# A two-layer decoder trunk on one core: element-wise work on another engine, and a plain down product in the last part of a feed-forward block

## The chip, the cores and the metric

One core of one Trainium2 chip runs the whole program. The metric is the device time of one execution in microseconds; less is better. Five engines work side by side, each in the order of its own queue, and wait for each other by semaphores: TensorE (PE in the profile; PEld is its loading of weights), VectorE (DVE), ScalarE (ACT), GpSimd (POOL) and SyncE (SP), which here only issues transfers. GpSimd can issue transfers too.

## The reference

A trunk of two layers on 512 positions of width 1024, in float32. Each layer is a feed-forward block, a group of token mixers, cross-attention into 256 memory positions, and a second feed-forward block.

```python
for l in range(DEPTH):                                    # DEPTH = 2
    x = x + 0.5 * swiglu(rms_norm(x, ffn1_norm[l]), w_gate, w_up, w_down)      # D_FF = 2816
    h = rms_norm(x, mix_norm[l])
    a_val, a_gate, b_gate, c_gate, b_h, q, k, v, q_idx, k_idx, w_idx = split(h @ w_in[l])
    y_a = conformer_conv(a_val, a_gate, ...)              # causal convolution over 31, layer norm
    y_b = short_gated_conv(b_gate, c_gate, b_h, ...)
    q, k, q_idx, k_idx = rope(q), rope(k), rope(q_idx), rope(k_idx)
    y_c = dsa_attention(q, k, v, q_idx, k_idx, w_idx)     # each position attends to its top 128 keys
    x = x + concat(y_a, y_b, y_c) @ w_out[l]
    x = x + memory_cross_attention(rms_norm(x, xa_norm[l]), rms_norm(mem, mem_norm[l]), ...)
    x = x + 0.5 * swiglu(rms_norm(x, ffn2_norm[l]), w_gate, w_up, w_down)
return rms_norm(x, final_norm)

def rms_norm(x, g): return x * rsqrt(mean(x * x) + 1e-6) * g
def swiglu(h, w_gate, w_up, w_down): return (silu(h @ w_gate) * (h @ w_up)) @ w_down
def rope(t): t1, t2 = halves(t); return concat(t1 * c - t2 * s, t2 * c + t1 * s)
```

## The kernel before

**Layout and precision.** Channels lie on the 128 partitions and the 512 positions on the free axis, so x is eight tiles X[0] to X[7] of 128 x 512 (line 483). A product in float32 is made of three fast passes: `split` (397) writes a rounded copy of a tile ("hi", by ScalarE) and the remainder ("lo", by VectorE), and `mm3` (410) adds hi·hi, hi·lo and lo·hi. Weights go the same way: a transfer into `stg`, then ScalarE writes `whi` and VectorE writes `wlo`. There are four buffers each of `stg`, `whi` and `wlo`, and two of `sum`.

**Feed-forward block (`ffn`, 624).** The 22 chunks of the hidden width are worked off in three parts of 8, 8 and 6 (`PARTS`, 48): a part makes its chunks (gate, up, silu, product) and then multiplies them down into X. Except for the first four chunks, these products use the scheme of Strassen and Winograd: two by two blocks of operands are combined so that seven products of 256 columns replace eight. `load_sevens` (541) brings the weights: three transfers on SyncE's queue, two on GpSimd's that add to what lies in the buffer, two additions on VectorE, and four splits. `Sevens.add` (588) combines the other operand with four operations on VectorE and four splits. `seven` (629) runs the products A to G, and the function `three` (746) and `fourth` (753) bring the results from PSUM into X with seven operations of 256 columns on VectorE and three copies on ScalarE for a pair of output chunks. The plain way is there too: with `by_sevens` false (665) the hidden chunks go into `Whole` (605), which only splits them, `load_quarters` (565) brings a chunk's weights with one transfer and one split, and each output chunk is 6 x 3 products of 512 columns and one operation that adds it to X (729 to 737). Before the change this path is taken in the last part of the last block of the kernel alone.

**Norms (`Norm`, 485).** As soon as a chunk of X is final, `chunk` (493) lets ScalarE square it, splits it with the gain for the next stage's product, and adds the square to a running sum (line 511, GpSimd). The next stage starts to multiply at once; `finish` and `rstd` (454) make 1/rms from the sum by products with ones, a power on GpSimd and a broadcast, and the result is multiplied in behind the product. The memory's norm (`mem_norm`, 817) does the same with four tiles inside the first block.

**Token mixers (`mix`, 886).** Projections run on TensorE one behind the other. Each of the eleven tiles per layer that take rope goes through `rope` (944) and `rotate` (911): ScalarE copies it out of PSUM, SyncE issues four transfers that swap its halves into a second tile, GpSimd multiplies that tile by the sines (912), VectorE multiplies the first by the cosines and adds the two (913, 914). Then `doubled` (917) copies heads between partitions by three transfers, and splits follow. Meanwhile VectorE works off the top-k search and the 31 taps of the convolution in the background (`some`). The attention of four pairs of heads, the memory's keys and values (`mem_kv`) and the output projection (`out_proj`, 865) follow; the latter multiplies plainly, and each chunk goes through `Norm.chunk`.

**Order.** Nothing is issued as it is written. `Plan` records every operation with a price (`price`, 238: GpSimd 0.1 us + 2.2 ns for each column, VectorE 0.068 us + 1/960 us for each) and the delay until other engines see it (`SEEN`, 178), gives each a due time counted back from TensorE's work, and issues all engines in the order of a simulated run (`order`, 270). Each engine keeps this order on the chip. So a changed price or engine can change the order of neighbours as well.

Of the kernel before, what the change touches and what calls it, by code (L numbers as in the profile page):

```python
# [361 lines left out]
def trunk_kernel(ctx: ExitStack, tc: tile.TileContext, a: dict, out: bass.AP):  # L362
# [6 lines left out]
    nc = Plan(tc)  # L369
# [15 lines left out]
    def slot(dt=F32, w=T):  # L385
        return planned(slots, "s", T, dt)[:, :w]
# [10 lines left out]
    def split(src, hi=None, lo=None, scale=None):  # L397

        w = src.shape[-1]
        if hi is None:  # L400
            hi, lo = slot(F32R, w), slot(F32R, w)
        if scale is None:
            nc.scalar.activation(hi, src, AF.Copy)
            nc.vector.tensor_sub(lo, src, f(hi))
        else:
            nc.scalar.activation(hi, src, AF.Copy, scale=scale)
            nc.vector.scalar_tensor_tensor(lo, src, scale, f(hi), op0=ALU.mult, op1=ALU.subtract)
        return hi, lo
# [41 lines left out]
    def pcol(name, i):  # L450
        return cols[:, COLS[name] + i:COLS[name] + i + 1]


    def rstd(sq, n, eps, rb=None, broadcast=True):


        nb = sq[0].shape[-1] // P
        ps = bank()
        for j in range(nb):
            for i, s in enumerate(sq):  # L460
                nc.tensor.matmul(ps[:, j:j + 1], s[:, j * P:(j + 1) * P], ones[:, 0:1],
                                 start=i == 0, stop=i == len(sq) - 1)
        v = sm(nb)
        nc.vector.tensor_scalar(v, ps[:, :nb], 1.0 / n, eps, op0=ALU.mult, op1=ALU.add)
        r = sm(nb)
        nc.gpsimd.tensor_tensor(r, v, mhalf[:, :nb], op=ALU.pow)
        if not broadcast:
            return r, None
        rhi, rlo = planned(small, "sm", 16, F32R)[:, :nb], sm(nb)
        nc.vector.tensor_copy(rhi, r)  # L470
        nc.vector.tensor_sub(rlo, r, f(rhi))
        pb = bank()
        for x in (f(rhi), rlo):
            dg = slot(F32R, nb * P)
            for j in range(nb):
                nc.vector.tensor_scalar(dg[:, j * P:(j + 1) * P], ident, x[:, j:j + 1], None, op0=ALU.mult)
            nc.tensor.matmul(pb[:, :nb * P], ones_r, dg, start=x is not rlo, stop=x is rlo)
        if rb is None:
            rb = slot(w=nb * P)
        nc.scalar.activation(rb, pb[:, :nb * P], AF.Copy)  # L480
        return r, rb
# [3 lines left out]
    class Norm:  # L485
# [7 lines left out]
        def chunk(self, c, x=slice(0, T)):  # L493
            sq = slot()[:, x]
            if self.floor is not None:
                nc.floor = self.floor + 2 * c
            if x.start:
                nc.vector.tensor_mul(sq, X[c][:, x], X[c][:, x])
            else:
                nc.scalar.activation(sq, X[c][:, x], AF.Square)  # L500
            nc.floor = -1e9
            if self.gain == "final_norm":
                if self.h[c] is None:
                    self.h[c] = slot()
                nc.vector.tensor_scalar(self.h[c][:, x], X[c][:, x], pcol(self.gain, c), None, op0=ALU.mult)
            else:
                self.h[c] = split(X[c], scale=pcol(self.gain, self.i * DC + c))
            if c == 0 or c == DC - 1 and self.gain == "final_norm":
                self.sq.append(sq)
            else:  # L510
                nc.gpsimd.tensor_add(self.sq[0][:, x], self.sq[0][:, x], sq)

        def finish(self, broadcast=True):
            self.r, self.rb = rstd(self.sq, D, 1e-6, broadcast=broadcast)
# [109 lines left out]
    def ffn(l, which, norm, nxt, begin=None, end=None):  # L624
# [37 lines left out]

        for f0, nf in PARTS:
            last = f0 + nf == FC
            by_sevens = not (end and last)
            hid, some = (Sevens if by_sevens else Whole)(), []

            def gated(pg, pu):
# [140 lines left out]
    def mem_part(c):  # L809

        t = slot()
        nc.behind = next(op for op in reversed(nc.ops) if op.eng == "tensor")
        nc.sync.dma_start(t, a["mem"][:, c * T:(c + 1) * T])
        nc.behind = None
        return t

    def mem_norm():
        for c in range(DC // 2):
            sq = slot()
            nc.scalar.activation(sq, mem_part(c), AF.Square)  # L820
            if c == 0:
                acc = sq
            else:
                nc.gpsimd.tensor_add(acc, acc, sq)
        rstd([acc[:, :M], acc[:, M:]], D, 1e-6, mrb)

    def mem_kv(l, kT, V):
# [58 lines left out]
    def mix(l, norm, nxt):  # L886
# [20 lines left out]
        cosr, sinr = slot(), slot()  # L907
# [1 line left out]
        nc.vector.tensor_mul(sinr, sin_t, norm.rb)  # L909

        def rotate(raw, swp):
            nc.gpsimd.tensor_mul(swp, swp, sinr)
            nc.vector.tensor_mul(raw, raw, cosr)
            nc.vector.tensor_add(raw, raw, swp)
            return raw
# [28 lines left out]
        def rope(o):  # L944
            raw, swp = slot(), slot()
            nc.scalar.activation(raw, o, AF.Copy)
            for q in range(4):
                s = q ^ 1
                nc.sync.dma_start(swp[q * 32:(q + 1) * 32], raw[s * 32:(s + 1) * 32])
            return rotate(raw, swp)  # L950
# [3 lines left out]
        for h in range(2):  # L954
            nc.sync.dma_start(kdup[h * 64:(h + 1) * 64], kraw[:64])
            for q in range(2):
                nc.sync.dma_start(kswp[h * 64 + q * 32:h * 64 + (q + 1) * 32], kraw[(1 - q) * 32:(2 - q) * 32])
        kdup = rotate(kdup, kswp)
        ki = high_low(kdup)
        qi = [queries(rope(o)) for o in oqi]  # L960
# [49 lines left out]
        acc = [None, None]  # L1010
# [271 lines left out]
    for l in range(L):  # L1282
        nxt = Norm("mix_norm", l)
        ffn(l, "ffn1", norm, nxt, begin if l == 0 else None)
        if l == 0:
            mem_norm()
        norm, nxt = nxt, Norm("xa_norm", l)
        kv = mix(l, norm, nxt)
        norm, nxt = nxt, Norm("ffn2_norm", l)
        cross(l, norm, nxt, kv)  # L1290
        norm, nxt = nxt, Norm("ffn1_norm" if l + 1 < L else "final_norm", l + 1)
        ffn(l, "ffn2", norm, nxt, end=end if l == L - 1 else None)
        norm = nxt
# [30 lines left out]
```

## Time and profile before

| | us |
|---|---|
| median of three runs | 2221.42 |
| lowest and highest | 2216.41, 2226.64 |
| the profiled execution | 2219.35 |
| its span, first to last instruction | 2217.6 |

The profile is of one execution. Its page gives busy times per engine; further views group instructions by line and shape, list who waited for whom, give busy times in chosen stretches, or list instructions in order of time. Nearly every instruction carries line 358, where the recorded operations are issued, so the rows are told apart by their tiles: `s` is a tile of the large pool, `ps` a bank of PSUM, `x` a tile of X, `sm` a small one, `cols` the gains; buffer numbers are left out. The table of busy times by stretch gives, behind the stretch and its length, the busy time and in brackets the count of instructions of PE, PEld, DVE, ACT and POOL, then TensorE's mean granted clock (1.00 is 2.4 GHz throughout), the share of the DMA engines and GB/s. A line of waits names the waiting engine and tile, what ended the wait, the sum in us, how often, and the longest. In time, the first feed-forward block lasts until about 362 us, the mixers of layer one until 655, cross-attention until 770, the second block until 1111; layer two's blocks and mixers end at about 1460, 1751, 1865 and 2203.

### The profile page before, as it was taken

Reading aid. Unit: us, or ns where it says so; the run is one execution under the profiler, and the core shown is the slowest. Engines: PE = TensorE matmul, PEld = TensorE weight load, DVE = VectorE, ACT = ScalarE, POOL = GpSimd, SP = SyncE. Lnnn points to the kernel's source line nnn. Section 1 sums busy time; section 2 is a strip of 40 time slices with the busy share of each in tenths; the row PEclk is TensorE's granted clock in tenths of the full one; section 3 lists DMA queues with packets and bytes.
Section 4 is the critical chain, followed back from the end, with each engine's and each line's share of the span. In section 5 each row is a group of like instructions: output and inputs, shape, how many; then the busy total and the mean of one; then the engine's idle time right before and its main releaser. Section 6 shows DMA issues by size and latency. Waiting matters only on the chain. (4 is left out here: it accounts for less than half of the span.)

```text
span 2217.6 us, 37769 instructions
## 1 busy us (share of the span) xinstructions
PE 2161.9 (97%) x14398; PEld 1974.7 (89%) x14398; DVE 1845.4 (83%) x3246; ACT 1205.7 (54%) x2039; POOL 355.1 (16%) x343
## 2 busy tenths in 40 slices
PE   9999999998999999999999999999989999999998
PEld 7999998787788889999989999978777888999997
DVE  8978888999965499888899887889998555988875
ACT  6656555336844456565656564643377344656553
POOL 3111114011020211111221111230100202111111
PEclk9999999999999999999999999999999999999999
DMA  6677766345332247776656777653543313577762
GB/s 189 165 177 181 179 166 170 111 127 148 105 105 67 76 111 189 176 183 179 158 127 163 195 174 188 150 160 96 142 122 109 103 48 97 138 180 182 185 165 74
DMA packets 133894, 319.29 MB, mean 144 GB/s; under 512 B 15184, under 2 KB 33232, under 8 KB 133712
## 3 DMA queue, kind: packets, MB, share of 16 engines
q1 hardware_dynamic: 100304, 257.62, 37.0%
q0 software_dynamic: 33408, 59.26, 18.2%
q8 instruction: 112, 1.84, 0.3%
q14 instruction: 70, 0.57, 0.1%
HBM read 300.57 MB, written 2.10 MB: 136 GB/s over the span
## 5 line engine op out<-in xcount | busy, mean ns | idle before, releaser
L358 PE MATMUL ps<-s,whi 128*128 128x256 f32 (+2 forms) x8592 | 1766.9, 309 | 12.3 <-ACT s L358 7.8
L358 PEld LDWEIGHTS ps<-s,whi 128*128 128x128 f32 (+1 forms) x8592 | 1358.0, 190 | 98.6 <-ACT s L358 12.5
L358 PE MATMUL ps<-s,wlo 128*128 128x256 f32 (+1 forms) x4296 | 1217.0, 308 | 10.6 <-DVE wlo L358 10.4
L358 PEld LDWEIGHTS ps<-s,wlo 128*128 128x128 f32 x4296 | 776.3, 190 | 53.2 <-DVE wlo L358 15.0
L358 ACT ACTIVATE whi<-stg 128x1024 fp32r<-128x1024 f32 (+1 forms) x398 | 413.0, 1042 | 464.9 <-PE ps L358 308.0
L358 DVE TENSOR_TENSOR wlo<-stg,whi 128x1024 fp32r<-128x1024 f32 (+1 forms) x398 | 480.2, 1208 | 93.8 <-ACT whi L358 85.3
L358 ACT ACTIVATE s<-ps 128x256 f32<-128x256 f32 (+5 forms) x576 | 238.5, 429 | 206.1 <-PE ps L358 200.9
L358 DVE TENSOR_TENSOR s<-s,s 128x512 fp32r<-128x512 f32 (+4 forms) x497 | 301.9, 627 | 10.3 <-ACT s L358 7.0
L358 ACT ACTIVATE s<-s 128x512 fp32r<-128x512 f32 (+3 forms) x401 | 225.5, 573 | 138.5 <-DVE s L358 90.9
L358 DVE TENSOR_TENSOR s<-ps,s 128x256 f32<-128x256 f32 (+2 forms) x352 | 179.2, 514 | 124.7 <-PE ps L358 104.5
L358 POOL TENSOR_TENSOR s<-s,s 128x512 f32<-128x512 f32 (+1 forms) x88 | 138.3, 1574 | 644.3 <-ACT s L358 387.9
L358 PE MATMUL ps<-s,s 128*128 128x512 f32 (+7 forms) x688 | 148.4, 370 | 21.0 <-DVE s L358 9.6
L358 PEld LDWEIGHTS ps<-s,s 128*128 128x128 f32 (+1 forms) x688 | 106.6, 185 | 50.6 <-DVE s L358 12.8
L358 ACT ACTIVATE whi<-s 128x512 fp32r<-128x512 f32 (+1 forms) x116 | 72.1, 621 | 123.7 <-PE ps L358 121.5
L358 DVE TENSOR_TENSOR wlo<-sum,whi 128x1024 fp32r<-128x1024 f32 (+1 forms) x116 | 138.5, 1194 | 0.0
L358 ACT ACTIVATE whi<-sum 128x1024 fp32r<-128x1024 f32 (+1 forms) x116 | 119.4, 1029 | 14.4 <-PE ps L358 12.4
L358 DVE SCALAR_TENSOR_TENSOR s<-s,cols,s 128x256 fp32r<-128x256 f32 (+13 forms) x144 | 104.5, 771 | 0.4
L358 DVE SCALAR_TENSOR_TENSOR s<-x,cols,s 128x512 fp32r<-128x512 f32 (+1 forms) x96 | 96.2, 1019 | 6.7 <-ACT s L358 5.1
L358 POOL DMA_DIRECT2D stg<-in_ffn_w_down x44 | 38.0, 863 | 353.5 <-DMA stg<-in_ffn_w_down 118.2
L358 DVE TENSOR_TENSOR wlo<-s,whi 128x512 fp32r<-128x512 f32 (+1 forms) x116 | 79.3, 684 | 15.8 <-ACT whi L358 15.2
L358 DVE TENSOR_TENSOR sum<-stg,stg 128x512 f32<-128x512 f32 (+1 forms) x116 | 79.1, 682 | 13.5 <-DMA stg<-in_ffn_w_up 8.0
L358 PE MATMUL ps<-whi,s 128*128 128x512 f32 x256 | 83.4, 398 | 0.0
(83 smaller groups left out, 1266.1 us busy)
## 6 DMA issues: line engine op xcount, KB each, us to landing
stg<-in_ffn_w_gate SPq DMA_DIRECT2D x86, 512.0 KB, 4.5
stg<-in_ffn_w_up SPq DMA_DIRECT2D x86, 512.0 KB, 4.9
stg<-in_ffn_w_down SPq DMA_DIRECT2D x64, 512.0 KB, 5.0
stg<-in_w_in SPq DMA_DIRECT2D x48, 512.0 KB, 3.7
stg<-in_xa_wkv SPq DMA_DIRECT2D x32, 512.0 KB, 4.0
stg<-in_ffn_w_down SPq DMA_DIRECT2D x32, 384.0 KB, 3.7
sum<-in_ffn_w_gate SPq DMA_DIRECT2D x36, 256.0 KB, 3.7
sum<-in_ffn_w_up SPq DMA_DIRECT2D x36, 256.0 KB, 4.0
```

What stands on the lines that cost most here:

```text
L358: getattr(getattr(nc, op.eng), op.name)(*map(real, op.args), **{k: real(v) for k, v in op.kw.items()})
```

## The change

Three additions or products move from GpSimd's queue to VectorE's: the running sum of squares in `Norm.chunk`, the same in `mem_norm`, and the product with the sines in `rotate`. And the condition for the seven-product way drops its first half: the last part (six chunks) of every feed-forward block now takes the plain path, where before only the last block of the kernel did.

```diff
--- before.py
+++ after.py
@@ -508,7 +508,7 @@
             if c == 0 or c == DC - 1 and self.gain == "final_norm":
                 self.sq.append(sq)
             else:
-                nc.gpsimd.tensor_add(self.sq[0][:, x], self.sq[0][:, x], sq)
+                nc.vector.tensor_add(self.sq[0][:, x], self.sq[0][:, x], sq)
 
         def finish(self, broadcast=True):
             self.r, self.rb = rstd(self.sq, D, 1e-6, broadcast=broadcast)
@@ -662,7 +662,7 @@
 
         for f0, nf in PARTS:
             last = f0 + nf == FC
-            by_sevens = not (end and last)
+            by_sevens = not last
             hid, some = (Sevens if by_sevens else Whole)(), []
 
             def gated(pg, pu):
@@ -821,7 +821,7 @@
             if c == 0:
                 acc = sq
             else:
-                nc.gpsimd.tensor_add(acc, acc, sq)
+                nc.vector.tensor_add(acc, acc, sq)
         rstd([acc[:, :M], acc[:, M:]], D, 1e-6, mrb)
 
     def mem_kv(l, kT, V):
@@ -909,7 +909,7 @@
         nc.vector.tensor_mul(sinr, sin_t, norm.rb)
 
         def rotate(raw, swp):
-            nc.gpsimd.tensor_mul(swp, swp, sinr)
+            nc.vector.tensor_mul(swp, swp, sinr)
             nc.vector.tensor_mul(raw, raw, cosr)
             nc.vector.tensor_add(raw, raw, swp)
             return raw
```

## Rows read from the trace of the kernel before

**Rows 1.** The page: span, and busy time by engine (share of span, instructions).
```profile
span 2217.6 us, 37769 instructions
...
PE 2161.9 (97%) x14398; PEld 1974.7 (89%) x14398; DVE 1845.4 (83%) x3246; ACT 1205.7 (54%) x2039; POOL 355.1 (16%) x343
```

**Rows 2.** Busy time by stretch: length; PE, PEld, DVE, ACT, POOL busy (count); clock, DMA, GB/s.
```profile
780.00:810.00 30.00, 30.00 (x134) 24.80 (x133) 29.57 (x59) 17.69 (x27) 1.79 (x2) 1.00 0.40 95
890.00:1010.00 120.00, 120.00 (x1000) 119.99 (x999) 101.17 (x167) 69.95 (x112) 20.44 (x24) 1.00 0.74 185
619.00:655.00 36.00, 36.00 (x160) 29.80 (x160) 23.76 (x22) 16.80 (x22) 9.41 (x6) 1.00 0.35 105
1088.00:1118.00 30.00, 27.50 (x199) 25.12 (x197) 29.97 (x50) 21.92 (x37) 13.71 (x11) 1.00 0.70 178
2177.00:2203.00 26.00, 26.00 (x141) 22.55 (x140) 15.04 (x20) 7.94 (x12) 7.17 (x6) 1.00 0.08 28
```

**Rows 3.** Waits, 1050 to 1125 us, TensorE's weight loads (PEld): sum, times, longest.
```profile
PEld ps L358 <- DVE wlo L358: 3.7, 4, 1.2
PEld ps L358 <- ACT s L358: 2.9, 4, 1.4
PEld ps L358 <- DVE s L358: 1.2, 2, 0.8
```

**Rows 4.** Waits of weight loads, 1376 to 1475 us.
```profile
PEld ps L358 <- DVE wlo L358: 4.8, 3, 2.2
PEld ps L358 <- ACT s L358: 2.2, 3, 1.4
```

**Rows 5.** Waits of weight loads, 243 to 366 us.
```profile
PEld ps L358 <- DVE wlo L358: 3.1, 4, 1.7
```

**Rows 6.** Waits of weight loads, 2108 to 2204 us, the plain block end.
```profile
PEld ps L358 <- ACT s L358: 0.8, 1, 0.8
```

**Rows 7.** Groups by shape, whole run: busy, mean ns | idle before, releasers.
```profile
L358 POOL TENSOR_TENSOR s<-s,s 128x512 f32<-128x512 f32 x86 | 136.8, 1593 | 640.9 <-ACT s L358 387.4 <-PE ps L358 173.9 <-DMA s<-s 54.2
...
L358 DVE TENSOR_TENSOR s<-s,s 128x512 f32<-128x512 f32 x108 | 79.2, 739 | 8.9 <-ACT s L358 6.6 <-POOL s L358 1.2
L358 DVE SCALAR_TENSOR_TENSOR s<-x,cols,s 128x512 fp32r<-128x512 f32 x64 | 73.3, 1154 | 6.7 <-ACT s L358 5.1
...
L358 DVE SCALAR_TENSOR_TENSOR s<-x,cols,s 128x512 f32<-128x512 f32 x32 | 22.9, 748 | 0.0
...
L358 DVE TENSOR_TENSOR wlo<-sum,whi 128x768 fp32r<-128x768 f32 x12 | 11.4, 951 | 0.0
...
L358 DVE TENSOR_TENSOR wlo<-s,whi 128x384 fp32r<-128x384 f32 x12 | 7.7, 641 | 0.0
...
L358 DVE TENSOR_TENSOR sum<-stg,stg 128x384 f32<-128x384 f32 x12 | 7.5, 624 | 0.0
```

**Rows 8.** Order of time, 13 to 20 us, VectorE: start, us, what.
```profile
16.46 1.78 DVE L358 SCALAR_TENSOR_TENSOR s<-x,cols,s 128x512 fp32r<-128x512 f32 x1
```

**Rows 9.** Order of time, 13 to 20 us, GpSimd.
```profile
11.76 9.33 POOL L358 TENSOR_TENSOR s<-s,s 128x512 f32<-128x512 f32 x6
```

**Rows 10.** Waits of weight loads, 5 to 35 us.
```profile
PEld ps L358 <- DVE s L358: 4.1, 4, 1.5
```

**Rows 11.** Order of time, 384 to 396 us, VectorE.
```profile
387.96 4.07 DVE L358 TENSOR_TENSOR s<-s,s 128x512 f32<-128x512 f32 x3
```

**Rows 12.** Waits of SyncE's queue, 381 to 400 us.
```profile
SPq L358 <- DVE s L358: 5.6, 3, 4.9
```

**Rows 13.** Waits of weight loads, 381 to 405 us.
```profile
PEld ps L358 <- ACT s L358: 2.2, 2, 1.4
```

**Rows 14.** Waits of weight loads, 505 to 530 us.
```profile
PEld ps L358 <- DVE s L358: 4.6, 2, 3.2
```

**Rows 15.** Busy time by stretch, 512 to 524 us, columns as in rows 2.
```profile
512.00:524.00 12.00, 7.53 (x33) 6.52 (x32) 11.67 (x32) 3.23 (x6) 2.84 (x3) 0.73 0.75 215
```

**Rows 16.** Order of time, 476 to 500 us, GpSimd.
```profile
482.72 8.14 POOL L358 TENSOR_TENSOR s<-s,s 128x512 f32<-128x512 f32 x2 [4.19 <-DMA s<-s]
```

## The prediction

> **What bounds the kernel now.** I read the busy times of the page first, then busy times by stretch, then who waited for whom in the stretches where TensorE is not full. The page puts TensorE at 97% of the span and VectorE at 83% [rows 1]; that alone says neither "TensorE-bound" nor where it isn't. The table by stretch does. In the middle of a feed-forward block 1000 products of 256 columns take 120.00 us, 0.120 us each, and its opening with products of 512 columns runs at 30.00 us / 133 weight loads = 0.226 us, with no idle time in either [rows 2]. These two paces are the prices of TensorE's work below. An output projection (619 to 655 us) is full too, 36.00 of 36, with VectorE at 23.76 [rows 2]. The picture turns at the end of a feed-forward block: from 1088 to 1118 us VectorE is busy 29.97 of 30 us and TensorE has holes, 27.50 of 30 [rows 2]. There VectorE sets the time. The same place in the last block of the kernel, whose last part already multiplies down plainly, has TensorE at 26.00 of 26 and VectorE at 15.04 [rows 2]. That block is this case's own sample of the second half of the change.
>
> So the 2162 us of TensorE work move only if its work or its holes change. I look for the holes, add what the change puts on TensorE, and ask which holes it closes.
>
> **Part 1: the last part multiplies down plainly (three blocks of four).** TensorE: a pair of output chunks costs 7 products x 3 chunk pairs x 3 passes = 63 matmuls of 256 columns, plainly 2 x 6 x 3 = 36 of 512. Per block of four pairs: 252 x 0.120 = 30.2 us against 144 x 0.226 = 32.5 us, +2.3; three blocks **+6.9 us**, all of it on the path, as TensorE is what is full.
> The Trainium skill's page "TensorE: Matmul & The Clock Gate" (section "Back-to-back issue gap") gives columns / 2.4 + 2.5 ns, 109 and 216 ns for these two. By it a block would go from 27.5 to 31.1 us and the three would cost +10.7, the sum 3.8 us more; the trace has 0.120 and 0.226, and I keep those.
>
> VectorE: the four kinds of work that only the seven-product load makes are, over the three blocks, remainders of the sums (12 x 0.951 = 11.4 us), of the fourth sum (7.7), and the two additions that make them (7.5, and a like row of 7.4): 34.0 us gone, 11.3 per block [rows 7]. The sums of hidden chunks and the extra evictions go too; I don't need their size, since the sample shows the whole. What VectorE has in the new 32.5 us: eight weight remainders of 0.95, eight evictions, eight splits of the next norm and seven added sums of squares at up to 0.75 each [rows 7]: 7.6 + 23 x 0.75 = 24.9 us, 77%. It stops being the bound, also with the added sums. The 24 accumulating transfers on GpSimd's queue and 12 of SyncE's go with the sums; nothing else stands in those queues then but the next stage's loads, which come no later.
>
> The holes. Weight loads waited, around the end of the blocks, 3.7 + 2.9 + 1.2 = 7.8 us [rows 3], 4.8 + 2.2 = 7.0 [rows 4] and 3.1 [rows 5], mostly for remainders of weights and for splits, the work above. In the plain sample the same stretch waited 0.8 us [rows 6]. What is late next would be the start of the following stage, where the last chunk's split must end before its product; the output projections have the same order of work, splits and sums included, and show no hole [rows 2]. So 17.9 - 3 x 0.8 = **-15.5 us**. Bounds: nothing, if the following stage only takes the wait over, and -17.9 if all holes close. I take the sample's value. Part 1: 6.9 - 15.5 = **-8.6 us**.
>
> **Part 2: 88 operations from GpSimd to VectorE.** They are 28 sums in output projections, 21 in the three block ends, 7 in the final norm, 7 at the start, 3 for the memory's norm, and 22 rope products. On GpSimd one takes 1.59 us, on VectorE at most 0.74 (this row's mean holds blocked ones) [rows 7]: 65 us more for VectorE if that were all. It isn't. A split with three operands takes 0.748 us where GpSimd rests (the row with f32 output) and 1.154 on the mean of the 64 that run beside these sums [rows 7], 26 us in all; at the start the two engines take turns, six GpSimd sums in 9.33 us while a split takes 1.78 [rows 8, 9], 1.03 more than 0.748. So each sum moved costs VectorE 0.74 and gives back up to 1.03. By place:
> - Output projections, final norm: VectorE has a third of the time free, TensorE is full [rows 2]. Zero.
> - Block ends: in part 1's sum already.
> - Memory's norm: inside the first block, beside full TensorE. Zero.
> - Start: seven sums, 7 x 0.74 = 5.2 us added against 7 x 1.03 = 7.2 given back. TensorE's loads waited 4.1 us for VectorE there [rows 10], so the 2.0 us are on the path: **-2 us** (bounds 0 and -4.1).
> - Early mixing: three rope products on GpSimd end one behind the other, VectorE needs 4.07 us for three operations that would take 2.2 alone [rows 11], SyncE stands 4.9 us until the rotated queries come [rows 12], and TensorE's loads wait 2.2 us [rows 13]. On VectorE the products cost 2.2 us and give 1.9 back there, and the chain loses GpSimd's 1.6 us for 0.74 three times. Bounds: 0, and the 2.2 of [rows 13]. I take **-2.5 us** for two layers (the second layer's hole is the smaller).
> - Late mixing: before the first attention TensorE's loads wait 4.6 us for VectorE [rows 14], and its granted clock falls to a mean of 0.73 between 512 and 524 us, a part of it at 1.2 instead of 2.4 GHz, behind that idle time [rows 15]. The rope chain leads there, but SyncE's copies and VectorE's order set most of it. One product in the chain is 0.85 us shorter. In one case GpSimd needed 8.14 us for two products, which busy VectorE held up [rows 16]. **-1 us** a layer, -2 together; bounds -5 and +3 a layer, the gain being the whole wait, the loss the eight products at 0.74 if nothing is given back (5.9) halved, since VectorE's background work there has slack.
>
> The Trainium skill's page "SBUF — State Buffer" (section "Who interferes with whom") has GpSimd instructions that read and VectorE instructions with two inputs exclude each other for a whole instruction. By it a sum moved would give back GpSimd's 1.56 us, and the start would gain 7 x (1.56 - 0.74) = 5.7 us, the sum 3.7 lower. The trace shows the exclusion, but 1.03 us of it.
>
> The written-out order is made anew: the planner prices such an operation at 0.10 + 512 x 0.0022 = 1.23 us on GpSimd and 0.068 + 512 / 960 = 0.60 on VectorE. Any stretch may be ordered otherwise; I give this +-4 us and no sign.
>
> **Sum.** -8.6 - 2 - 2.5 - 2 = -15.1 us on the profiled execution's 2219.35 (span 2217.6): 2204.3. That execution lies 2.1 us under the median of 2221.42, so the forecast is **2206 us**.
>
> **Rivals.**
> 1. The holes at the block ends don't close, because the transfers or the next stage's first split set them: part 1 is +6.9, the total -15.1 + 15.5 = about 0, 2222 us. For it: loads of the next stage run there at the same time. Against: the releasers are VectorE's and ScalarE's work, and VectorE is 29.97 of 30 busy; the sample has no holes. Chance 0.17.
> 2. Slower: VectorE takes over GpSimd's wait for the half-swapped copies. GpSimd waited 54.2 us for them [rows 7]; VectorE works in order, and behind a rope product stand convolution taps, top-k steps and remainders of weights for TensorE. If all came over: 2206 + 54 = 2260 us. It decides from 15 + 11 = 26 us of such waits on, 1.2 us for each of the 22. Against: the addition behind the product, which needs the same copy, waited for GpSimd 1.2 us in the whole kernel [rows 7]; the copies land well ahead. Chance 0.08.
> 3. More than forecast: in late mixing the wait shrinks so far that the clock stays up, -5 a layer instead of -1, and the start gains all of its wait: -15.1 - 8 - 2 = 2196 us. Chance 0.15.
> 4. That the change doesn't do what it says: one line selects the plain path that the last block already runs; 0.
>
> **How the numbers follow.** Forecast (2199 to 2214) 0.60, rivals as above. The range leaves out the tails of rivals 2 and 3 and part of 1: 2191 to 2222. 0.5% is 11 us, about what a measurement of this kernel can tell from no change. Under 2210.3: most of the forecast's 0.60 (0.52) and all of rival 3 (0.15), 0.67. Over 2232.5: rival 2's larger half and chance reorderings, 0.07. Between: 0.26.
>
> **What would show it.** Block ends: TensorE full, VectorE near 77%, waits of weight loads about 1 us per block instead of 7; three stretches 2.3 us longer in TensorE's own work. Splits of the norms near 0.75 us instead of 1.15. GpSimd left with its transfers and the powers, under 210 us. Wrong would be: waits of VectorE for the copies in rope (rival 2), or new holes at the first product of the stage behind a block (rival 1). A late-mixing wait that grew would say that the order made anew, not the operations, moved the time.

## The result and the profile after

The changed kernel takes 2189.63 us (median of four runs, 2188.61 to 2192.77) against 2220.35 us for the kernel before beside it (2216.41 to 2226.64): ratio 0.9861, interval 0.9836 to 0.9887. That is 30.7 us less. The forecast was 15 us less (2206, range 2191 to 2222): the sign was right, the size half of what came, and the median lies 1.4 us under the range.

The page of the profile after, as in [rows 1]:

```profile
span 2187.8 us, 36566 instructions
...
PE 2156.3 (99%) x14074; PEld 1962.0 (90%) x14074; DVE 1777.7 (81%) x3172; ACT 1170.7 (54%) x1960; POOL 194.1 (9%) x231
```

TensorE now idles 31.5 us of the span, before it was 55.7. GpSimd fell from 355 to 194 us, under the 210 that I had named. TensorE's busy time is no fixed quantity: the moves alone, told of below, have the same 14398 products as the kernel before and keep TensorE busy 2154.7 us, not 2161.9.

Busy time by stretch, columns as in [rows 2]: the middle of a block, the end of layer one's second block (the counterpart of 1088 to 1118 us before), the end of the first block, and the start.

```profile
860.00:980.00 120.00, 120.00 (x1000) 120.00 (x999) 101.02 (x167) 69.84 (x111) 20.61 (x24) 1.00 0.73 183
1053.00:1095.00 42.00, 42.00 (x219) 36.11 (x218) 28.19 (x40) 21.71 (x32) 0.86 (x1) 1.00 0.50 136
314.00:342.00 28.00, 28.00 (x150) 24.26 (x149) 17.97 (x27) 13.73 (x21) 0.86 (x1) 1.00 0.50 132
0.00:51.90 51.90, 50.28 (x232) 42.43 (x233) 45.27 (x93) 33.29 (x55) 6.88 (x15) 1.00 0.67 210
```

The pace of TensorE's products is the same 0.120 us. At the block ends it is full (42.00 of 42), and VectorE, 29.97 of 30 before, is at 28.19 of 42, 67%. Weight loads show no wait at all there, where [rows 3 to 5] stood. Around the start and the early mixing, waits of weight loads from 5 to 35 us (first row) and from 365 to 396 us (the others; the place lies 12 us earlier than before, and its counterpart, 377 to 408 us, has waits of 3.4 us before):

```profile
PEld ps L358 <- ACT s L358: 0.7, 1, 0.7
...
PEld ps L358 <- issue: 0.4, 1, 0.4
PEld ps L358 <- ACT s L358: 0.2, 1, 0.2
```

So most of the 4.1 us of [rows 10] and of the 2.2 us of [rows 13] is gone too. The groups by shape (columns as in [rows 7]):

```profile
L358 DVE TENSOR_TENSOR s<-s,s 128x512 f32<-128x512 f32 x194 | 130.1, 683 | 5.3 <-ACT s L358 4.1
L358 DVE SCALAR_TENSOR_TENSOR s<-x,cols,s 128x512 fp32r<-128x512 f32 x64 | 47.6, 747 | 5.3 <-ACT s L358 5.3
```

The norms' splits take 747 ns instead of 1154, and the sums and products that moved are in the first group: 194 instead of 108, and the mean is *shorter*, 683 instead of 739 ns. Rival 2 is answered in the same row: this group, with the rope products in it, idled 5.3 us in the whole run, 4.1 of them for ScalarE, so at most 1.2 us for swapped copies, not 54.

Where the time came from, in us. The stages are cut at the first product of a long row of equal products (the 256-column ones of a block, the 512-column ones of late mixing and of the output projection), the same cuts in all kernels. "Forecast" is my terms put into these stages: a block end is +2.3 and its holes; of the early mixing's 2.5 I put 1.5 into layer one. The last two columns are runs told of below, against the moves alone.

| stage | before | forecast | after | plain product alone | moves alone | GpSimd reads behind rope | behind sums |
|---|---|---|---|---|---|---|---|
| start | 55.6 | -2.0 | -3.7 | -0.1 | -3.8 | +0.3 | +6.9 |
| layer 1, first block, early mixing | 352.2 | -1.5 | -8.2 | -3.1 | -6.6 | +1.1 | +8.2 |
| layer 1, late mixing | 203.1 | -1.0 | -2.6 | -1.1 | -3.6 | +7.7 | +2.0 |
| layer 1, second block | 346.2 | -4.7 | -5.7 | -4.1 | -6.0 | -0.2 | +9.9 |
| layer 2, first block, early mixing | 344.8 | -4.9 | -7.8 | -5.8 | -8.9 | +4.1 | +6.2 |
| layer 2, late mixing | 202.5 | -1.0 | -3.7 | -0.2 | -2.3 | +9.8 | +0.6 |
| the rest | 713.2 | 0 | +1.9 | +0.7 | +0.9 | -1.8 | -1.7 |
| span | 2217.6 | -15.1 | -29.8 | -13.8 | -30.4 | +21.3 | +32.1 |

(One execution each, so a cell can be off by a microsecond or two; the medians are with the experiments. A change of order alone can move a single cell by 6 us without moving the median, as the experiments on order show.)

### The profile page after: what moved, and what is told of

Its sections match the earlier page's. It is cut to its first block, busy times and chain, and to the rows that moved or that the text cites. A ratio compares the mean times of both kernels' runs of the same rounds, so it can differ in the third digit from the quotient of the medians.

```text
span 2187.8 us, 36566 instructions
## 1 busy us (share of the span) xinstructions
PE 2156.3 (99%) x14074; PEld 1962.0 (90%) x14074; DVE 1777.7 (81%) x3172; ACT 1170.7 (54%) x1960; POOL 194.1 (9%) x231
## 4 chain that ended last, share of the span: by engine, by line
PE 78%; DVE 17%; issue 2%; DMA 2%; ACT 1%; SPq 0%; DVEq 0%; POOLq 0%; POOL 0%; ACTq 0%
PE ps L358 78%; DVE s L358 11%; DVE wlo L358 4%; DVE sm L358 2%; DMA s<-s 1%; ACT s L358 1%; DMA stg<-in_ffn_w_down 0%; DMA stg<-in_ffn_w_gate 0%; DVE sum L358 0%; DMA x<-in_x 0%; SPq L358 0%; ACT L358 0%; ACT whi L358 0%; DVEq L358 0%; POOLq L1320 0%
## 5 line engine op out<-in xcount | busy, mean ns | idle before, releaser
L358 PE MATMUL ps<-s,whi 128*128 128x256 f32 (+1 forms) x8376 | 1758.7, 313 | 5.3 <-ACT s L358 3.2
L358 PEld LDWEIGHTS ps<-s,whi 128*128 128x128 f32 x8376 | 1336.3, 190 | 99.5 <-ACT s L358 5.8
L358 DVE TENSOR_TENSOR s<-s,s 128x512 f32<-128x512 f32 (+3 forms) x558 | 330.9, 613 | 6.8 <-ACT s L358 4.1
L358 ACT ACTIVATE s<-ps 128x256 f32<-128x256 f32 (+3 forms) x540 | 223.6, 431 | 189.2 <-PE ps L358 186.9
L358 ACT ACTIVATE whi<-s 128x512 fp32r<-128x512 f32 x104 | 65.7, 632 | 114.1 <-PE ps L358 111.8
L358 DVE TENSOR_TENSOR wlo<-sum,whi 128x1024 fp32r<-128x1024 f32 x104 | 126.5, 1216 | 0.0
L358 ACT ACTIVATE whi<-sum 128x1024 fp32r<-128x1024 f32 x104 | 109.2, 1050 | 12.9 <-PE ps L358 11.0
L358 DVE SCALAR_TENSOR_TENSOR s<-s,cols,s 128x256 fp32r<-128x256 f32 (+11 forms) x144 | 94.8, 700 | 0.4
L358 DVE TENSOR_TENSOR wlo<-s,whi 128x512 fp32r<-128x512 f32 x104 | 71.1, 684 | 19.8 <-ACT whi L358 19.1
L358 DVE TENSOR_TENSOR sum<-stg,stg 128x512 f32<-128x512 f32 x104 | 70.9, 682 | 5.9 <-DMA stg<-in_ffn_w_down 4.4
```

Of the source, the lines that this page charges most:

```text
L358: getattr(getattr(nc, op.eng), op.name)(*map(real, op.args), **{k: real(v) for k, v in op.kw.items()})
```

## Experiments

The question was which half of the change closes the holes at the block ends and where the rest of the gain comes from. Three theories stood against each other. Contention: a GpSimd instruction that reads from SBUF, the memory of the tiles, holds up VectorE's instructions with two inputs there, and taking it off frees the *urgent* ones. The plain product: fewer instructions on VectorE at the block ends. Order (theory C): the new engines and prices give another written-out order, and that made the difference. (The letters A and B in the expectations mean something else from run to run; each says what.) The kernel before, run beside them, had medians of 2216.1 to 2217.3 us.

**The parts by themselves.** The line of `by_sevens` alone (`not last`), the three moved operations alone, and of these the two sums alone and the rope product alone:

```diff
-            by_sevens = not (end and last)
+            by_sevens = not last                                                     # e1 only
-                nc.gpsimd.tensor_add(self.sq[0][:, x], self.sq[0][:, x], sq)
+                nc.vector.tensor_add(self.sq[0][:, x], self.sq[0][:, x], sq)             # e2, e3; mem_norm too
-            nc.gpsimd.tensor_mul(swp, swp, sinr)
+            nc.vector.tensor_mul(swp, swp, sinr)                                     # e2, e4
```

> The plain down product in the last parts alone, the sums and rope products left on GpSimd. Theory A (the holes at the three block ends come from VectorE's work for the seven products): they close although the sums stay on GpSimd, TensorE has 7.3 us more of its own work, about 22 us of holes go: 13 to 16 us faster than before, start and mixing unchanged. Rival B (the blocking by GpSimd's sums made the holes): half of the holes stay, 3 us slower to 5 us faster.

> The three moves to VectorE alone, seven products kept everywhere. Theory A: start 3.7 us, early mixing about 5 and late mixing about 6 us faster, and at the block ends little (VectorE stays full there: it gains 7 times 0.3 us each): 15 to 18 us faster in all. Rival B: the block ends close as well, 25 to 30 us faster, nearly the whole change. If both parts close the same holes, the gains of this run and of the plain product alone add up to more than 30.7 us.

> Only the sums of squares on VectorE, rope products on GpSimd, seven products everywhere. Start 3 to 4 us faster; block ends 0 to 2 us each; output projections 0, as TensorE is full there; mixing unchanged. 4 to 8 us faster by theory A, 12 to 20 by rival B (blocking by the sums made the holes at the block ends).

> Only the rope products on VectorE. If the gain in mixing comes from them: 8 to 11 us faster, all of it in the two mixing stages (early holes of about 2.5 us each gone, the wait ahead of the first attention 2 to 4 us shorter), start and block ends unchanged. If the mixing stages gained from another order of the queues that the rest of the change brought: under 3 us, or slower.

Measured, medians of four runs each: plain product alone 2206.39 us (0.9954, 0.9939 to 0.9969), 10.3 less; moves alone 2189.78 (0.9882, 0.9864 to 0.9900), 26.9 less; sums alone 2199.09 (0.9919, 0.9904 to 0.9934), 17.6 less; rope alone 2208.17 (0.9960, 0.9945 to 0.9975), 8.5 less. The plain product brought less than the 13 to 16 us of its theory A and more than the 5 of its rival; the moves alone and the sums alone came out as rival B had it, against theory A; rope lies in its range. Sums and rope add up (26.1 against 26.9). Plain product and moves do not: 10.3 + 26.9 = 37.2, but the whole change has 30.7 beside its own kernel before, and its median equals that of the moves alone (the two were not run beside each other). With the plain product alone the norms' splits still take 1138 ns, yet no weight load waits at the second block's end: there fewer instructions did it. So both are cures for the same holes, and the moves suffice.

How the moves alone do it is the lesson. Moves alone, busy time by stretch at the second block's end, still with the seven products, and placed as 1088 to 1118 us in [rows 2] (22 us ahead of the end of the row of 256-column products):

```profile
1070.00:1100.00 30.00, 29.56 (x223) 28.19 (x222) 30.00 (x59) 22.92 (x39) 3.57 (x5) 1.00 0.72 182
```

VectorE is as full as before (30.00 of 30), yet TensorE went from 27.50 to 29.56, and VectorE did 59 instructions in 30 us instead of 50. In the whole run it has 88 instructions more than before and is busy 1833.9 us instead of 1845.4:

```profile
PE 2154.7 (99%) x14398; PEld 1974.8 (90%) x14398; DVE 1833.9 (84%) x3334; ACT 1200.9 (55%) x2038; POOL 215.1 (10%) x255
```

Here is what had held it up, in the kernel before, in order of time (start, us, engine): two sums on GpSimd, VectorE's instructions beside them, and TensorE's weight load that waited.

```profile
1114.74 3.22 POOL L358 TENSOR_TENSOR s<-s,s 128x512 f32<-128x512 f32 x2 [1.49 <-ACT s L358]
...
1113.89 1.21 DVE L358 TENSOR_TENSOR wlo<-stg,whi 128x1024 fp32r<-128x1024 f32 x1
1115.02 1.79 DVE L358 SCALAR_TENSOR_TENSOR s<-x,cols,s 128x512 fp32r<-128x512 f32 x1
1116.74 2.30 DVE L358 TENSOR_TENSOR wlo<-stg,whi 128x1024 fp32r<-128x1024 f32 x1
...
1119.09 0.19 PEld L358 LDWEIGHTS ps<-s,wlo 128*128 128x128 f32 x1 [1.24 <-DVE wlo L358]
```

The remainder of a weight takes 1.21 us, and 2.30 beside GpSimd's second sum; the split before it 1.79 instead of 0.74. The weight load behind this remainder stood 1.24 us for it, one of the four waits in the first row of [rows 3]. And with the sums on VectorE (moves alone, the same place):

```profile
1091.21 0.68 DVE L358 TENSOR_TENSOR s<-s,s 128x512 f32<-128x512 f32 x1
...
1097.48 0.74 DVE L358 SCALAR_TENSOR_TENSOR s<-x,cols,s 128x512 fp32r<-128x512 f32 x1
1098.14 0.68 DVE L358 TENSOR_TENSOR s<-s,s 128x512 f32<-128x512 f32 x1
1098.75 2.35 DVE L358 TENSOR_TENSOR wlo<-stg,whi 128x1024 fp32r<-128x1024 f32 x2
1101.02 0.68 DVE L358 TENSOR_TENSOR s<-s,s 128x512 f32<-128x512 f32 x1
1101.62 1.21 DVE L358 TENSOR_TENSOR wlo<-stg,whi 128x1024 fp32r<-128x1024 f32 x1
1102.76 0.68 DVE L358 TENSOR_TENSOR s<-s,s 128x512 f32<-128x512 f32 x1
1103.36 1.21 DVE L358 TENSOR_TENSOR wlo<-stg,whi 128x1024 fp32r<-128x1024 f32 x1
1104.49 0.68 DVE L358 TENSOR_TENSOR s<-s,s 128x512 f32<-128x512 f32 x1
```

Nobody needs the sums until the norm is finished, so the planner puts the first of the block's seven at 1091.21 us, 1.1 us ahead of the end of the row of 256-column products, and four of them behind the last split (1097.48), between remainders. On GpSimd the first ran 14.7 us ahead of that end, and each as soon as its square was there, and took up to a microsecond from whatever VectorE was doing. In the whole kernel before, 64 instructions of VectorE took over 0.1 us longer than the median of their shape in the moves alone, 61.6 us in all, and each of them overlaps a sum or product of 512 columns on GpSimd. In the moves alone and in the kernel after there is none.

**The reads put back.** To the moves alone, a two-input instruction of the same size was added on GpSimd behind each moved one; nobody reads its result, so this is extra work. Then the same behind the rope products only, and behind the sums only:

```diff
                 nc.vector.tensor_add(self.sq[0][:, x], self.sq[0][:, x], sq)
+                nc.gpsimd.tensor_add(sq, sq, X[c][:, x])        # e5, e15; in mem_norm tensor_add(sq, sq, sq)
...
             nc.vector.tensor_add(raw, raw, swp)
+            nc.gpsimd.tensor_mul(swp, swp, cosr)                # e5, e14
```

> The three moves alone (run e2_moves, 2189.8 us), and GpSimd is given an operation of the old size and kind behind each moved one (two inputs in SBUF, 512 columns), whose result nobody reads. The chains stay on VectorE; only the work beside it comes back. Theory A (VectorE is blocked while GpSimd reads): start 3 us, block ends 4 us each, mixing 2 to 4 us per layer slower again, 2203 to 2215 us, and the splits of the norms back over 1.1 us. Theory B (what helped was that sums and products are ready sooner): within 4 us of e2_moves.

> The three moves alone, and behind each of the 22 rope products on VectorE a product of the same size on GpSimd whose result nobody reads. Theory (a GpSimd reading instruction holds up VectorE's two-input work, and costs time where that work is urgent): the late mixing of both layers gets longer by 9.5 and 6.4 us, as with the reads behind all moved operations, early mixing by 3 to 5 in all, the rest not: 16 to 22 us over the moves alone, 2206 to 2212 us. Rival (it is the sums that matter, rope has slack): under 6 us more, at most 2196.

> The three moves alone, and behind each moved sum of squares on VectorE a sum of the same size on GpSimd whose result nobody reads. Theory: the start gets longer by 7 us, the first block by 8 to 10, the ends of the two other blocks by 5 and 3, late mixing not: 22 to 30 us over the moves alone, 2212 to 2220 us, and with the run that has the reads behind rope it adds up to the 47.7 us of both. Rival (the rope products matter, sums can be put off): under 8 us more, at most 2198. If the two runs together stay 10 us or more under 47.7, the reads hold each other up and the cost is not one by place.

All reads: 2237.48 us (1.0096, 1.0072 to 1.0121), 47.7 over the moves alone and far past the 2203 to 2215 expected, although VectorE's and TensorE's instructions are the same ones and TensorE's stand in nearly the same order. The splits, expected over 1.1 us again, took 831 ns: the reads now stand behind VectorE's sums and meet other instructions. Behind rope alone: 2206.42 (0.9960, 0.9945 to 0.9974), 16.6 over. Behind the sums alone: 2216.00 (0.9997, 0.9987 to 1.0008), 26.2 over. Together 42.8 of 47.7: nearly additive, both medians within what was expected. By stage (last columns of the table) the sums' reads cost time at the start and in the blocks (in the second block, 9.9 us, more than expected) and little in late mixing, the rope's nearly the reverse. Part of the price is TensorE's clock: over the start with the sums' reads, 58.7 us, TensorE idled 4.8 us and its mean granted clock was 0.94; in the moves alone, 51.8 us, it idled 1.4 at 1.00. Groups by shape, with reads behind the sums:

```profile
L358 POOL TENSOR_TENSOR s<-s,x 128x512 f32<-128x512 f32 x61 | 93.2, 1530 | 390.3 <-DVE s L358 375.1 <-issue 4.9 <-PE ps L358 4.4
...
L358 DVE TENSOR_TENSOR s<-s,s 128x512 f32<-128x512 f32 x194 | 144.4, 758 | 6.7 <-ACT s L358 5.6
L358 DVE SCALAR_TENSOR_TENSOR s<-x,cols,s 128x512 fp32r<-128x512 f32 x64 | 53.0, 831 | 4.9 <-ACT s L358 4.9
```

Splits and sums are lengthened again (831 and 758 ns against 744 and 683 with the moves alone). For late mixing, the stage as a whole: before, moves alone, reads behind rope (columns as in [rows 2]):

```profile
407.90:611.00 203.10, 191.34 (x970) 155.31 (x968) 197.18 (x426) 109.79 (x222) 17.55 (x9) 0.97 0.43 120
...
397.40:597.00 199.60, 190.91 (x969) 155.22 (x967) 196.06 (x434) 109.26 (x222) 1.01 (x1) 0.97 0.41 121
...
398.80:606.00 207.20, 194.01 (x968) 157.40 (x966) 202.99 (x434) 109.59 (x222) 20.14 (x9) 0.95 0.40 116
```

This stage is VectorE's: it is busy 197.18 of 203.10 us. Eight products more left its busy time 1.1 us *shorter*; GpSimd's reads brought it 6.9 us back with not one instruction more, and the stage grew by 7.6.

**Writing without reading.** The same places, with a fill of 512 columns on GpSimd instead of the two-input instruction (`nc.gpsimd.memset(sq, 0.0)`, `nc.gpsimd.memset(swp, 0.0)`), whose result nobody reads either.

> Like e5_dummy, but the operation given to GpSimd only writes (it fills the same 512 columns with zero), in the same order of the queues. If any GpSimd work on SBUF blocks VectorE's operations with two inputs: 3 to 10 us slower than e2_moves, in proportion to its length. If only reading blocks: within 2 us of e2_moves, and splits at 0.75 us.

Measured 2188.85 us (0.9873, 0.9852 to 0.9895): no difference from the moves alone. This run and the one with all reads have the same instructions of TensorE and of VectorE in the same order from end to end, so the 48.6 us between them come from GpSimd's instruction and not from an order. Groups by shape:

```profile
L358 POOL MEMSET s<- 128x512 f32 x86 | 45.9, 534 | 716.3 <-DVE s L358 677.3 <-DVE sm L358 13.5 <-PE ps L358 13.3
...
L358 DVE SCALAR_TENSOR_TENSOR s<-x,cols,s 128x512 fp32r<-128x512 f32 x64 | 47.5, 745 | 4.9 <-ACT s L358 4.9
```

So it is not that GpSimd has something in its queue, but that its instruction reads. The fill is shorter too (534 ns, the reading sums 1530 in the mean), but 78 of VectorE's instructions with no input from PSUM overlap a fill, and none of them is longer by more than 0.02 us. The Trainium skill's page "SBUF — State Buffer" (section "Who interferes with whom") says just this: a VectorE instruction with two inputs in SBUF contends with a GpSimd instruction that reads SBUF, not with one that only writes it. The trace agrees, with 534 ns fills beside unchanged splits.

**Order.** Five runs ask what a new order alone does: the planner told GpSimd's 1.23 us for all moved operations on VectorE, the same for the rope products alone, a planner constant (`SLACK`, 0.05 to 0.07) changed in the moves alone and in the kernel before, and the kernel before with GpSimd's operations priced like VectorE's:

```diff
-        op.cost = 0.96 if n < 16 else 0.1 + n * 2.2e-3
+        op.cost = 0.96 if n < 16 else 0.068 + n / 960              # e8, GpSimd's price in the kernel before
...
+            if self.slow:                                           # e6 around all moved operations, e13 around rope
+                op.cost = 0.1 + n * 2.2e-3
```

> The three moves alone, but the planner is told GpSimd's old price for them (1.23 us instead of 0.60), so that the queues come out in another order for the same work. If the order made anew carries the gain (theory C): 8 us or more slower than e2_moves. If it doesn't: 2186 to 2194 us, within 4 us of it.

> The three moves alone, with GpSimd's old price told to the planner for the rope products only, the sums at their own price. In e6_price both were told wrong, and 17 us were lost, 9 of them ahead of the attention. If a product that the plan takes for longer than it is puts everything behind it in the chain late: the mixing stages lose the same 9 us here, and the blocks nothing, 2197 to 2201 us. If e6_price only hit an unlucky order: within 4 us of e2_moves.

> The three moves alone, with the planner's safety margin at 0.07 instead of 0.05 us: the same work, other orders of the queues on all engines. It measures what an order alone is worth. If the gain of the moves is the work (theory A): within 5 us of e2_moves (2189.8 us). If a lucky order made it (theory C): 8 us or more slower.

> The kernel before with the same margin of 0.07: the same question for it. Theory A: within 5 us of before (2216 us), and so 20 us or more over e11_slack. Theory C: the distance between the two kernels shrinks under 15 us.

> The kernel before, all work left on GpSimd, but the planner prices GpSimd's element-wise operations like VectorE's (0.60 us instead of 1.23). Theory C (order): 8 us or more faster than before. Theory A: within 5 us of before, either sign, since VectorE is blocked as much as ever.

Measured: all moved operations overpriced 2206.76 us (2200.00 to 2209.16; 0.9948, 0.9927 to 0.9969), 17 us over the moves alone; rope alone overpriced 2192.79 (2192.09 to 2198.75; 0.9891, 0.9870 to 0.9911), 3 over and not the 7 to 11 of a chain put late; `SLACK` 2191.23 (0.9878, 0.9862 to 0.9894) and 2217.89 (1.0005, 0.9994 to 1.0016), within 1.5 of their partners; GpSimd underpriced 2221.70 (1.0022, 1.0011 to 1.0032), 5.6 over, where theory C had 8 less. A neutral disturbance of the order is worth 1 to 2 us in the median, so order by itself did not bring 27. In a single stage it is worth more: the kernel before with `SLACK` 0.07 has 346 us for layer one's first block with early mixing, 6 less than without and about as little as the moves alone (by the same cuts), and loses them again elsewhere. So the gain in that cell of the table is not shown to be contention. And a wrong price can lose most of the whole gain, with all other things equal, and theory C has that much right. Why the sums' wrong price costs so much more than the rope's stays open: the two were not run apart beyond this.

**The plain product everywhere.** What do its columns cost where no hole is to be closed? The whole change with `by_sevens = False`, eight more parts of eight chunks:

> The changed kernel with the plain down product in all three parts of every block. In the first two parts TensorE is full and there is nothing to close: 192 x 0.227 - 336 x 0.120 = 3.3 us more for each of eight parts, 26 us slower than the changed kernel, about 2216 us. If lighter VectorE work pays in the middle of a block as well: less than 15 us slower.

2209.71 us (0.9966, 0.9955 to 0.9977), 20 over the whole change (23 by the ratios, each to the kernel before beside it), less than the 26 expected and more than the rival's 15. By my price a part of eight chunks costs 4 pairs x (48 x 0.226 - 84 x 0.120) = 3.1 us more, eight of them 24.6. The price holds to four fifths or better.

**A version that might beat both.** In the profile after, the largest hole left lies in late mixing, at the norm behind the convolution. That norm called one pair of heads earlier, on the moves alone and on the whole change:

```diff
-            if hp == NH // 2 - 1:
+            if hp == NH // 2 - 2:
```

> The three moves alone, with the norm behind the convolution called one pair of heads earlier in both layers. Theory (the hole of some 4.5 us a layer at that norm is on the path, since TensorE is full before and behind it): 4 to 9 us less than the moves alone, 2181 to 2186 us. Rival (the taps of the convolution on VectorE are not done by then, so the hole only moves ahead or a wait for the taps takes its place): within 3 us of the moves alone, 2187 to 2193, or slower.

> The whole change, with the norm behind the convolution called one pair of heads earlier in both layers. Theory: 4 to 9 us less than the whole change, 2181 to 2186 us, the same as the moves alone with this edit, since the plain product adds nothing on top of the moves. Rival (the hole only moves): 2187 to 2193.

2199.03 us (0.9923, 0.9906 to 0.9941) and 2202.10 (0.9937, 0.9918 to 0.9955): 9 and 12 *slower* than without, where the theory had 4 to 9 less. Moves alone from 550 to 590 us, then with the earlier norm from 550 to 570:

```profile
550.00:570.00 20.00, 20.00 (x101) 15.19 (x101) 19.94 (x41) 18.02 (x42) 0.00 (x0) 1.00 0.37 117
570.00:590.00 20.00, 16.02 (x65) 11.07 (x64) 18.37 (x38) 11.95 (x31) 1.01 (x1) 0.87 0.25 79
...
550.00:570.00 20.00, 14.99 (x54) 9.54 (x53) 19.94 (x38) 5.98 (x9) 0.00 (x0) 0.88 0.25 80
```

The hole moved 20 us ahead and grew from 4.0 to 5.0 us, and VectorE is full in it (19.94 of 20): the convolution's taps are not done by then, the last of them ends at 569.9 us. From 497 to 620 us as a whole TensorE idled 11.8 us instead of 8.7, at a mean granted clock of 0.94 instead of 0.96. My theory that this hole is a matter of order fell; it is VectorE's work. No version here beats the moves alone and the whole change, which these runs don't tell apart.

## Why the forecast was right in sign and half in size

The miss is 14.7 us (29.8 against 15.1 on the span): by the table 6.7 in layer one's first block with early mixing, 4.3 in late mixing, 2.9 in layer two's first block, 1.7 at the start, 1.0 in the second block, less 1.9 in the rest.

The step that failed is part 2, which priced the moved operations place by place as a cost less a gift: 6.5 us in all, where the moves alone brought 26.9. Its zeros ("Block ends: in part 1's sum already") and its small terms for the start, early and late mixing were too low. Part 1 by itself came near: 8.6 forecast, 10.3 measured with the plain product alone. In the whole change the miss is smaller than part 2's own, because both parts close the same holes at the block ends.

- **Plain product on TensorE, +6.9.** About right: where nothing is to close, the same price gave 24.6 and the chip 20 to 23. Most of it is on the path.
- **Holes at the block ends, -15.5, put down to the plain product.** Place and sign right, cause only half. The step "Block ends: in part 1's sum already" priced the moved sums at nothing there. They close the holes without the plain product (second block -6.0 against -4.1). With VectorE at 29.97 of 30 I should have asked which of its instructions were stretched: the trace had remainders of 2.30 us where others took 1.21.
- **The size of the holes.** Where a hole ends in the stage that I looked at, waits of weight loads did well: the second block gained 5.7 + 2.3 = 8.0 against the 7.8 of [rows 3]. In layer one's first block I took one row of the view [rows 5] for the whole. Three others there have 0.8, 0.6 and 0.3 us, and all of it closed, the 0.8 that I left as in the sample too: 2.5 us. The first two parts of that block, where I put nothing, gained 3.1: counted from the block's first product, the 2160th starts after 268.9 us before and after 265.8 now, with 1.3 of it won by the 100th. These 3.1 are not contention on the spot, since from 31 to 341 us GpSimd has no sum or product in the kernel before; by the run with `SLACK` 0.07 an order alone can bring as much. (The memory's three sums, which I placed inside this block, ran at its end or behind it: the ten sums there start between 341.6 and 373.6 us.) Early mixing adds 1.3 (below). Together that is the 6.7, to 0.2 us.
- **"Each sum moved costs 0.74 and gives back up to 1.03".** Both figures are near the measured ones (0.68, and 1.79 - 0.74 = 1.05 or 2.30 - 1.21 = 1.09), but subtracting one from the other was the mistake. The cost falls where the planner puts the sum, the gift where VectorE was held up, and these are different moments. At the start, where I subtracted, VectorE was busy 47.78 us with 85 instructions before (the row below) and 45.27 with 93 after, and the stage gained 3.7, close to my bound of 4.1, not 2.

```profile
0.00:55.60 55.60, 52.03 (x232) 42.67 (x233) 47.78 (x85) 35.41 (x59) 17.03 (x22) 1.00 0.62 189
```

- **Early mixing, -2.5.** Too low; by the waits it is -4.7: those of weight loads fell from 3.4 to 0.6 us in layer one, where I put 1.5 and bounded by the one row of [rows 13], and from 2.4 to 0.5 in layer two, where I put 1.0.
- **Late mixing, -1 a layer.** -2.6 and -3.7, inside the bounds of -5 and +3. The step that failed is "VectorE's background work there has slack": I read the holes of TensorE and not the stage's busy time, which has VectorE at 97%. Rival 3 had the direction, not the mechanism: the granted clock of the whole stage is 0.97 in both layers before, and 0.97 and 0.98 after.
- **Block ends' VectorE share, 77%.** It is 67% in the 42 us that I looked at; I had priced every instruction at its upper bound.
- **Rival 1** (holes stay) fell: no waits of weight loads there. **Rival 2** (waits for the copies) fell: at most 1.2 us. **The order, +-4 without a sign**: fair for a neutral change, too small for a wrong price.
- **The rest, 0.** It is 1.9 us longer, 1.1 of it behind VectorE's last instruction, where only the final transfers run (4.5 us before, 5.6 after). The change does not touch them; the cause is open.

The interval I gave was too narrow on the low side because its lower end let only late mixing and the start gain more, and no case let all the places gain at once. They did. For the start, the block ends and late mixing the runs with GpSimd's reads show one cause; for the opening of the first block it stays open.

## What to carry to other kernels

An instruction on a "free" engine is not free if it holds up another engine: look for one shape with two durations (here 747 and 1154 ns, 1.21 and 2.30 us) and see what ran beside the long ones. When such work is moved onto the full engine, don't subtract its cost from what it frees; ask for each *when* it falls: here work that could be put off cost little on an engine that was full only in places. And when two edits both cure the stretch where an engine is full, expect one cure's worth, not the sum.

## What the runs showed of the hardware

A GpSimd instruction that reads 512 columns twice took 1.28 to 1.30 us at its shortest (at 1098.70 and 1101.57 us of the kernel before) and lengthened the VectorE instruction that it met by 0.4 to 1.1 us; one that only writes took 0.53 us and lengthened nothing. How much is lost follows from when the two meet. In order of time, kernel before:

```profile
1098.70 1.28 POOL L358 TENSOR_TENSOR s<-s,s 128x512 f32<-128x512 f32 x1 [1.71 <-ACT s L358]
1101.57 1.30 POOL L358 TENSOR_TENSOR s<-s,s 128x512 f32<-128x512 f32 x1 [1.60 <-ACT s L358]
...
1098.99 1.40 DVE L358 TENSOR_TENSOR sum<-stg,stg 128x384 f32<-128x384 f32 x1
...
1101.65 0.41 DVE L358 TENSOR_TENSOR s<-ps,s 128x256 f32<-128x256 f32 x1
1101.98 1.71 DVE L358 TENSOR_TENSOR wlo<-stg,whi 128x768 fp32r<-128x768 f32 x1
```

At 1098.99 GpSimd had 0.98 us left, and VectorE took 1.40 instead of 0.55, 0.85 longer; at 1101.98 it had 0.89 left, and the remainder took 1.71 instead of 0.95, 0.76 longer. So VectorE waits for what is left of GpSimd's instruction, all but 0.13 us, and then does its own work in full. In 61 of the 64 lengthened instructions GpSimd had started first, and the rule holds for each of them, all but 0.13 to 0.20 us; in the other three GpSimd started up to 0.06 us later. The 1.03 that the prediction set against "a whole instruction" was such a rest. Two inputs are not the whole condition: the final norm's scaling by a column, with one tile as input, took 1.60 us instead of 0.49 at 2190.99. The instruction at 1101.65, with an input from PSUM, kept its time, as did all 14 with such an input that began while GpSimd's instruction ran.

The holding up goes both ways. With reads behind rope a single GpSimd product took 5.22 us beside VectorE's instructions, in order of time:

```profile
487.90 5.22 POOL L358 TENSOR_TENSOR s<-s,s 128x512 f32<-128x512 f32 x1 [4.28 <-DVE s L358]
...
488.35 1.28 DVE L358 TENSOR_TENSOR s<-s,s 128x512 fp32r<-128x512 f32 x2
489.56 1.21 DVE L358 TENSOR_TENSOR wlo<-stg,whi 128x1024 fp32r<-128x1024 f32 x1
490.69 1.28 DVE L358 TENSOR_TENSOR s<-s,s 128x512 f32<-128x512 f32 x2
491.89 1.77 DVE L358 SCALAR_TENSOR_TENSOR s<-s,cols,s 128x504 f32<-128x504 f32 x1
```

The section of the Trainium skill named above calls the shared ports an exclusive lock, under which the other engine blocks fully instead of being slowed. The trace agrees: the 61 rests above are waits in full. Five instructions of VectorE with two inputs in SBUF, back to back, kept their usual times while GpSimd stood; then GpSimd's product ran and the next of VectorE took 1.77 instead of 0.73. Why VectorE kept its turn here for five instructions and in other places for none, no run tells.
